# Row blocks of 112 and 16 for 1, 111 and 16 in a relu and row-sum kernel

## Chip, cores, metric

One core of one Trainium2 chip. The metric is device time in microseconds (us) of one execution, median of several; the span of a profile is about 1.4 us shorter than the time of its run. All runs told here are of the fast state, at a granted clock of 1.0. In the profile's lines SPq is the queue that issues the DMA transfers, ACT is ScalarE and DVE is VectorE. A load has landed when the last part of its data is in; a chunk is 16 rows per partition.

## The reference

The input x has the shape 32 x 512 x 1024 in float32, 16,384 rows of 1024 numbers, 67.1 MB.

```python
def reference(x: np.ndarray) -> np.ndarray:
    relu_x = np.maximum(x, 0)
    return np.sum(relu_x, axis=-1).astype(np.float32)
```

## The kernel before

The rows are laid on 128 partitions, 128 rows each. Which rows a partition gets is set by REGIONS: a block of n rows per partition takes 128 n consecutive rows of the input, and partition p the n rows from p x n of them. Before, there were three blocks of 1, 111 and 16 rows. So the very first load, one row per partition, is one contiguous piece of 512 KB. The price is that the sums of those 128 rows lie in one column, 4 bytes in each of 128 partitions, while the output has them side by side. The kernel transposes that column on VectorE and stores it as 4 pieces of 128 bytes.

```python
REGIONS = [1, 111, 16]
CHUNKS = [[(0, 0, 1), (1, 0, 15)]] + [[(1, 16 * c + 15, 16)] for c in range(6)]
# ... (block, first row, rows): chunk 0 is two loads, chunks 1 to 6 are one each
    xv = [
        xr[P * s : P * (s + n), :].rearrange("(p j) d -> p j d", p=P)
        for s, n in zip(start, REGIONS)
    ]
# ... three buffers of 16 rows; a load waits until VectorE has summed the chunk three before
    for c in range(NBIG + 1):
        if c >= NB:
            sp.wait_ge(s_dve, done[c - NB])
        if c < NBIG:
            i = 0
            for g, j, n in CHUNKS[c]:
                sp.dma_start(
                    out=buf[:, c % NB, i : i + n, :], in_=xv[g][:, j : j + n, :]
                ).then_inc(s_in[c], 16)
                i += n
# ... the loads of chunk 0 are moved ahead of the first barrier; tail loads of 8, 4, 2 rows;
# ... the last two rows come in four pieces, one of them (the end of the one row and the
# ... start of the other) into a tile of its own, "seam"
    sp.wait_ge(s_turn, 1)
    sp.dma_start(
        out=of[0:P].rearrange("(k q) -> k q", q=32), in_=turned[0:P:32, 0:32]
    ).then_inc(s_store, 16)
    sp.wait_ge(s_fact, 1)
    sp.wait_ge(s_fdve, 1)
    sp.wait_ge(s_in[-1], 16)
    sp.dma_start(out=ov[1][:, :], in_=res[:, start[1] : start[2]]).then_inc(s_store, 16)
# ... ScalarE applies relu to a chunk in place, VectorE sums its rows in steps:
        if c == 1:
            dve.wait_ge(s_dve, done[c])
            dve.transpose(out=turned[:, :], in_=res[:, 0:32]).then_inc(s_turn, 1)
```

Of the kernel before, what the change touches and what calls it, by code (L numbers as in the profile page):

```python
# [3 lines left out]
P = 128  # L4
D = 1024
BIG = 16
NB = 3
REGIONS = [1, 111, 16]
CHUNKS = [[(0, 0, 1), (1, 0, 15)]] + [[(1, 16 * c + 15, 16)] for c in range(6)]
ACT_STEPS = [[16], [7, 9], [7, 9], [7, 9], [4, 5, 7], [3, 4, 5]]  # L10
DVE_STEPS = [[4, 5, 7], [7, 4, 5], [7, 4, 5], [7, 4, 5], [4, 5, 7], [3, 4, 5]]
TAIL = [8, 4, 2]
CUT = 912
HEAD = 256


def bass_relu_sum_kernel(
# [1 line left out]
    x: bass.AP,  # L19
    out: bass.AP,  # L20
):




# [6 lines left out]
    fp32 = mybir.dt.float32  # L32
# [5 lines left out]
    J = B * S // P  # L38
    NBIG = len(CHUNKS)
    assert BIG * NBIG + sum(TAIL) + 2 == J == sum(REGIONS)  # L40

    xr = x.rearrange("b s d -> (b s) d")
    of = out.rearrange("b s -> (b s)")
    start = [sum(REGIONS[:i]) for i in range(len(REGIONS))]
# [4 lines that stand above are left out]
    ov = [of[P * s : P * (s + n)].rearrange("(p j) -> p j", p=P) for s, n in zip(start, REGIONS)]  # L49

    buf = nc.alloc_sbuf_tensor("buf", [P, NB, BIG, D], fp32)
    w = D - CUT
    seam = nc.alloc_sbuf_tensor("seam", [P, 2 + w + HEAD + 2], fp32)
    res = nc.alloc_sbuf_tensor("res", [P, J], fp32)
    turned = nc.alloc_sbuf_tensor("turned", [P, 32], fp32)

    n_in = NBIG + len(TAIL) + 3
    s_in = [nc.alloc_semaphore(f"s_in{i}") for i in range(n_in)]
# [1 line left out]
    s_dve = nc.alloc_semaphore("s_dve")  # L60
    s_fact = nc.alloc_semaphore("s_fact")
    s_fdve = nc.alloc_semaphore("s_fdve")
    s_half = nc.alloc_semaphore("s_half")
    s_seam = nc.alloc_semaphore("s_seam")
    s_last = nc.alloc_semaphore("s_last")
    s_turn = nc.alloc_semaphore("s_turn")
    s_store = nc.alloc_semaphore("s_store")
    s_out = nc.alloc_semaphore("s_out")

    sp, act, dve = nc.sync, nc.scalar, nc.vector  # L70

    NTWO = len(ACT_STEPS)
    done = [sum(map(len, DVE_STEPS[: c + 1])) for c in range(NTWO)]

# [10 lines left out]
# [8 lines that stand above are left out]
# [14 lines left out]

    rows = xv[-1].rearrange("p j d -> p (j d)")[:, r * D : (r + 2) * D]
    flat = buf[:, tb, r : r + 2, :].rearrange("p j d -> p (j d)")
    first, second, third = [(0, CUT), (D + D // 2, 2 * D), (D + HEAD, D + D // 2)]  # L110
    for k, (lo, hi) in enumerate((first, second, third)):
        sp.dma_start(out=flat[:, lo:hi], in_=rows[:, lo:hi]).then_inc(  # L112
            s_in[NBIG + len(TAIL) + k], 16
        )
    sp.dma_start(out=seam[:, 2 : 2 + w + HEAD], in_=rows[:, CUT : D + HEAD]).then_inc(s_seam, 16)
    sp.wait_ge(s_turn, 1)
    sp.dma_start(
        out=of[0:P].rearrange("(k q) -> k q", q=32), in_=turned[0:P:32, 0:32]
    ).then_inc(s_store, 16)
    sp.wait_ge(s_fact, 1)  # L120
    sp.wait_ge(s_fdve, 1)
    sp.wait_ge(s_in[-1], 16)
    sp.dma_start(out=ov[1][:, :], in_=res[:, start[1] : start[2]]).then_inc(s_store, 16)


    def on_act(t, acc):
        return act.activation(t, t, AF.Relu, accum_out=acc)  # L127

    def on_dve(t, acc):
        return dve.tensor_scalar(  # L130
            out=t, in0=t, scalar1=0.0, scalar2=None, op0=ALU.max, op1=ALU.add, accum_out=acc
        )

    def row(c, i):
        return buf[:, c % NB, i, :], res[:, c * BIG + i : c * BIG + i + 1]

    k = 0
    for c in range(NTWO):
        alone = BIG - sum(ACT_STEPS[c])
        act.wait_ge(s_in[c], 16 * len(CHUNKS[c]))  # L140
        r = 0
        ready = []
        for n in ACT_STEPS[c]:
            t = buf[:, c % NB, r : r + n, :]
            act.activation(t, t, AF.Relu).then_inc(s_act, 1)  # L145
            k += 1
            ready += [k] * n
            r += n
        for i in range(BIG - alone // 2, BIG):
            on_act(*row(c, i))  # L150
        if alone:
            dve.wait_ge(s_in[c], 16 * len(CHUNKS[c]))
            for i in range(BIG - alone, BIG - alone // 2):
                on_dve(*row(c, i))
        r = seen = 0
        for n in DVE_STEPS[c]:
            if ready[r + n - 1] > seen:
                seen = ready[r + n - 1]
                dve.wait_ge(s_act, seen)
            dve.tensor_reduce(  # L160
                out=res[:, c * BIG + r : c * BIG + r + n],
                in_=buf[:, c % NB, r : r + n, :],
                axis=X,
                op=ALU.add,
            ).then_inc(s_dve, 1)
            r += n
        if c == 1:
            dve.wait_ge(s_dve, done[c])
            dve.transpose(out=turned[:, :], in_=res[:, 0:32]).then_inc(s_turn, 1)  # L169


    j0 = NBIG * BIG
    for c in range(NTWO, NBIG):
        act.wait_ge(s_in[c], 16 * len(CHUNKS[c]))
        dve.wait_ge(s_in[c], 16 * len(CHUNKS[c]))
        for i in range(BIG):
# [10 lines left out]
    lo, hi = first  # L187
    act.wait_ge(s_in[-3], 16)
    dve.wait_ge(s_in[-3], 16)
    on_act(flat[:, lo : CUT // 2], seam[:, 0:1]).then_inc(s_half, 1)  # L190
    on_dve(flat[:, CUT // 2 : hi], seam[:, 1:2]).then_inc(s_half, 1)
    k = 2 + w
    lo, hi = second
    act.wait_ge(s_in[-2], 16)
    on_act(flat[:, lo:hi], seam[:, k + HEAD : k + HEAD + 1]).then_inc(s_seam, 1)
    lo, hi = third
    dve.wait_ge(s_in[-1], 16)
    on_dve(flat[:, lo:hi], seam[:, k + HEAD + 1 : k + HEAD + 2]).then_inc(s_seam, 1)
    act.wait_ge(s_seam, 16 + 2)
    act.wait_ge(s_half, 2)  # L200
    on_act(seam[:, 0:k], res[:, J - 2 : J - 1]).then_inc(s_last, 1)
    dve.wait_ge(s_seam, 16 + 2)
    on_dve(seam[:, k : k + HEAD + 2], res[:, J - 1 : J]).then_inc(s_last, 1)


    sp.wait_ge(s_last, 2)
    sp.dma_start(out=ov[-1][:, :], in_=res[:, start[-1] : J]).then_inc(s_out, 16)
    sp.wait_ge(s_store, 16 * (len(REGIONS) - 1))
    sp.wait_ge(s_out, 16)
# [28 lines left out]
```

## Time and profile before

| | before |
|---|---|
| time, median of 6 runs (range) | 160.83 us (160.75 to 161.05) |
| span of the profile | 159.4 us |
| first chunk landed | 21.61 us |
| mean step between the landings of chunks 0 to 6 | 19.35 us for 8.39 MB |
| last store issued | 157.93 us |

The rows that carry these, and how they are read, are in the prediction. This is the time of the first load from issue to landing (last column), from the page's list of DMA issues of the kernel before:

```profile
buf<-in_x_dram SPq DMA_DIRECT2D x1, 512.0 KB, 3.3
```

And these are the packets that the DMA began in the first 3 us of the span:

```profile
DMA packets 160, 1.51 MB, mean 502 GB/s; under 512 B 16, under 2 KB 16, under 8 KB 144
```

### The profile page before, as it was taken

The numbers are of one execution on the slowest core, as the hardware profiler recorded it, in microseconds if no ns is written. First come the engines' busy times: TensorE is split into PE (matmuls) and PEld (weight loads), VectorE is DVE, ScalarE is ACT, GpSimd is POOL, SyncE is SP. The second block draws the span as 40 slices with busy tenths as digits, with TensorE's granted clock in tenths as the row PEclk, the third lists the DMA queues.
The fourth block names the chain that finished last, engine by engine and source line by source line (L and its number), as shares of the span: only waits on it lengthen the run. The fifth ranks groups of instructions, "written<-read, shape, count | busy, mean of one in ns | idle before, by whom it ended". The sixth has DMA issues, their size and how long they took to land.

```text
span 159.4 us, 150 instructions
## 1 busy us (share of the span) xinstructions
DVE 120.6 (76%) x59; ACT 101.5 (64%) x54; POOL 0.2 (0%) x4
## 2 busy tenths in 40 slices
DVE  0000000009999999999999999999999999898995
ACT  3000059980799708996099941999329980496975
POOL 0000000000000000000000000000000000000000
DMA  9997996996996997989979969969969979798994
GB/s 378 493 401 339 493 526 263 526 526 263 526 493 296 526 444 345 526 378 411 526 312 477 526 263 526 526 263 526 526 263 526 444 345 526 321 469 374 417 400 142
DMA packets 2457, 67.18 MB, mean 421 GB/s; under 512 B 536, under 2 KB 792, under 8 KB 1176
## 3 DMA queue, kind: packets, MB, share of 16 engines
q1 hardware_dynamic: 2456, 67.18, 98.1%
q14 instruction: 1, 0.01, 0.0%
HBM read 67.11 MB, written 0.07 MB: 421 GB/s over the span
## 4 chain that ended last, share of the span: by engine, by line
DVE 55%; DMA 34%; ACT 9%; SPq 2%; issue 0%
DVE res L160 54%; DMA buf<-in_x_dram 34%; ACT buf L145 9%; SPq L101 1%; SPq L112 1%; DVE buf L130 0%; DVE seam L130 0%; SPq L91 0%; DVE turned L169 0%
## 5 line engine op out<-in xcount | busy, mean ns | idle before, releaser
L160 DVE TENSOR_REDUCE res<-buf 128x4 f32<-128x4096 f32 (+3 forms) x18 | 99.4, 5596 | 35.5 <-ACT buf L145 35.5
L145 ACT ACTIVATE buf<-buf 128x7168 f32<-128x7168 f32 (+5 forms) x13 | 80.4, 6233 | 46.1 <-DMA buf<-in_x_dram 46.1
L127 ACT ACTIVATE buf<-buf 128x1024 f32<-128x1024 f32 (+2 forms) x19 | 19.0, 999 | 8.9 <-DMA buf<-in_x_dram 8.9
L130 DVE TENSOR_SCALAR_CACHE_REDUCE buf<-buf 128x1024 f32<-128x1024 f32 (+2 forms) x19 | 20.7, 1143 | 1.7 <-DMA buf<-in_x_dram 1.6
L127 ACT ACTIVATION_READ_ACCUMULATOR buf<-buf 128x1 f32 x19 | 3.6, 188 | 0.0
L145 ACT ACT_TABLE_LOAD x1 | 1.3, 1283 | 1.3 <-PEq L223 1.3
L130 DVE DVE_READ_ACCUMULATOR buf<-buf 128x1 f32 x19 | 1.6, 84 | 0.0
L130 DVE TENSOR_SCALAR_CACHE_REDUCE seam<-seam 128x258 f32<-128x258 f32 x1 | 0.4, 421 | 0.0
L127 ACT ACTIVATE seam<-seam 128x114 f32<-128x114 f32 x1 | 0.3, 300 | 0.1
L169 DVE STREAM_TRANSPOSE turned<-res 128x32 f32<-128x32 f32 x1 | 0.2, 211 | 0.0
L127 ACT ACTIVATION_READ_ACCUMULATOR seam<-seam 128x1 f32 x1 | 0.2, 186 | 0.0
L223 POOL MEMSET const-bfloat16-1.0<- 128x1 bf16 x1 | 0.1, 101 | 0.0
L223 POOL MEMSET const-uint8-127<- 128x1 uint8 x1 | 0.1, 101 | 0.0
L223 POOL MEMSET const-float32-0.0<- 128x1 f32 x1 | 0.1, 98 | 0.2 <-issue 0.2
L223 POOL MEMSET const-float32-1.0<- 128x1 f32 x1 | 0.1, 98 | 0.0
L130 DVE DVE_READ_ACCUMULATOR seam<-seam 128x1 f32 x1 | 0.1, 82 | 0.0
## 6 DMA issues: line engine op xcount, KB each, us to landing
buf<-in_x_dram SPq DMA_DIRECT2D x1, 7680.0 KB, 21.1
buf<-in_x_dram SPq DMA_DIRECT2D x1, 4096.0 KB, 25.3
buf<-in_x_dram SPq DMA_DIRECT2D x1, 2048.0 KB, 29.9
buf<-in_x_dram SPq DMA_DIRECT2D x1, 1024.0 KB, 31.9
buf<-in_x_dram SPq DMA_DIRECT2D x1, 512.0 KB, 3.3
buf<-in_x_dram SPq DMA_DIRECT2D x1, 456.0 KB, 32.5
buf<-in_x_dram SPq DMA_DIRECT2D x1, 256.0 KB, 32.7
seam<-in_x_dram SPq DMA_DIRECT2D x1, 184.0 KB, 32.6
```

The source lines that it names most:

```text
L101: sp.dma_start(out=buf[:, tb, r : r + n, :], in_=xv[-1][:, r : r + n, :]).then_inc(s_in[NBIG + i], 16)
L112: sp.dma_start(out=flat[:, lo:hi], in_=rows[:, lo:hi]).then_inc(s_in[NBIG + len(TAIL) + k], 16)
L127: return act.activation(t, t, AF.Relu, accum_out=acc)
L130: return dve.tensor_scalar(out=t, in0=t, scalar1=0.0, scalar2=None, op0=ALU.max, op1=ALU.add, accum_out=acc)
L145: act.activation(t, t, AF.Relu).then_inc(s_act, 1)
L160: dve.tensor_reduce(out=res[:, c * BIG + r : c * BIG + r + n], in_=buf[:, c % NB, r : r + n, :], axis=X, op=ALU.add,).then_inc(s_dve, 1)
L169: dve.transpose(out=turned[:, :], in_=res[:, 0:32]).then_inc(s_turn, 1)
L223: nc = _bacc.Bacc("TRN2", target_bir_lowering=False, num_devices=1)
```

## The change

The intent: a simpler layout, with one block of 112 rows and no column that needs transposing, and pieces of the last two rows that begin and end on multiples of 512 bytes. The first load is still one row per partition, but of 112; its 128 pieces of 4 KB now lie 448 KiB apart.

```diff
-REGIONS = [1, 111, 16]
-CHUNKS = [[(0, 0, 1), (1, 0, 15)]] + [[(1, 16 * c + 15, 16)] for c in range(6)]
+REGIONS = [112, 16]
+CHUNKS = [[(0, 0, 1), (0, 1, 15)]] + [[(0, 16 * c, 16)] for c in range(1, 7)]
-DVE_STEPS = [[4, 5, 7], [7, 4, 5], [7, 4, 5], ...
+DVE_STEPS = [[4, 5, 7], [3, 4, 4, 5], [7, 4, 5], ...
-CUT = 912
+CUT = 896
+MID = 512                      # the same place as D // 2 before
-    seam = nc.alloc_sbuf_tensor("seam", [P, 2 + w + HEAD + 2], fp32)
+    z = 96
+    seam = nc.alloc_sbuf_tensor("seam", [P, z + w + HEAD + 2], fp32)
-    sp.dma_start(out=seam[:, 2 : 2 + w + HEAD], in_=rows[:, CUT : D + HEAD]).then_inc(s_seam, 16)
-    sp.wait_ge(s_turn, 1)
-    sp.dma_start(
-        out=of[0:P].rearrange("(k q) -> k q", q=32), in_=turned[0:P:32, 0:32]
-    ).then_inc(s_store, 16)
+    sp.dma_start(out=seam[:, z : z + w + HEAD], in_=rows[:, CUT : D + HEAD]).then_inc(s_seam, 16)
-    sp.dma_start(out=ov[1][:, :], in_=res[:, start[1] : start[2]]).then_inc(s_store, 16)
+    sp.dma_start(out=ov[0][:, :], in_=res[:, 0 : start[1]]).then_inc(s_store, 16)
-        if c == 1:
-            dve.wait_ge(s_dve, done[c])
-            dve.transpose(out=turned[:, :], in_=res[:, 0:32]).then_inc(s_turn, 1)
...                             # the tile and semaphore of the transpose, and seam offsets
```

More of the change, by code (lines that the diff above doesn't have):

```diff
@@ L7 @@
 NB = 3
-REGIONS = [1, 111, 16]
-CHUNKS = [[(0, 0, 1), (1, 0, 15)]] + [[(1, 16 * c + 15, 16)] for c in range(6)]
+REGIONS = [112, 16]
+CHUNKS = [[(0, 0, 1), (0, 1, 15)]] + [[(0, 16 * c, 16)] for c in range(1, 7)]
 ACT_STEPS = [[16], [7, 9], [7, 9], [7, 9], [4, 5, 7], [3, 4, 5]]
-DVE_STEPS = [[4, 5, 7], [7, 4, 5], [7, 4, 5], [7, 4, 5], [4, 5, 7], [3, 4, 5]]
+DVE_STEPS = [[4, 5, 7], [3, 4, 4, 5], [7, 4, 5], [7, 4, 5], [4, 5, 7], [3, 4, 5]]
 TAIL = [8, 4, 2]
-CUT = 912
+CUT = 896
 HEAD = 256
+MID = 512
 def bass_relu_sum_kernel(
@@ L52, in bass_relu_sum_kernel @@
     w = D - CUT
-    seam = nc.alloc_sbuf_tensor("seam", [P, 2 + w + HEAD + 2], fp32)
+    z = 96
+    seam = nc.alloc_sbuf_tensor("seam", [P, z + w + HEAD + 2], fp32)
     res = nc.alloc_sbuf_tensor("res", [P, J], fp32)
-    turned = nc.alloc_sbuf_tensor("turned", [P, 32], fp32)
     n_in = NBIG + len(TAIL) + 3
@@ L65, in bass_relu_sum_kernel @@
     s_last = nc.alloc_semaphore("s_last")
-    s_turn = nc.alloc_semaphore("s_turn")
     s_store = nc.alloc_semaphore("s_store")
@@ L109, in bass_relu_sum_kernel @@
     flat = buf[:, tb, r : r + 2, :].rearrange("p j d -> p (j d)")
-    first, second, third = [(0, CUT), (D + D // 2, 2 * D), (D + HEAD, D + D // 2)]
+    first, second, third = [(0, CUT), (D + MID, 2 * D), (D + HEAD, D + MID)]
     for k, (lo, hi) in enumerate((first, second, third)):
@@ L189, in bass_relu_sum_kernel @@
     dve.wait_ge(s_in[-3], 16)
-    on_act(flat[:, lo : CUT // 2], seam[:, 0:1]).then_inc(s_half, 1)
-    on_dve(flat[:, CUT // 2 : hi], seam[:, 1:2]).then_inc(s_half, 1)
-    k = 2 + w
+    on_act(flat[:, lo : CUT // 2], seam[:, z - 2 : z - 1]).then_inc(s_half, 1)
+    on_dve(flat[:, CUT // 2 : hi], seam[:, z - 1 : z]).then_inc(s_half, 1)
+    k = z + w
     lo, hi = second
@@ L200, in bass_relu_sum_kernel @@
     act.wait_ge(s_half, 2)
-    on_act(seam[:, 0:k], res[:, J - 2 : J - 1]).then_inc(s_last, 1)
+    on_act(seam[:, z - 2 : k], res[:, J - 2 : J - 1]).then_inc(s_last, 1)
     dve.wait_ge(s_seam, 16 + 2)
```

## The prediction

> **What bounds the kernel now.** I read the page first, then the queue's own waits, then the order of instructions on each engine. On the page:
>
> ```profile
> span 159.4 us, 150 instructions
> DVE 120.6 (76%) x59; ACT 101.5 (64%) x54; POOL 0.2 (0%) x4
> ...
> DMA packets 2457, 67.18 MB, mean 421 GB/s; under 512 B 536, under 2 KB 792, under 8 KB 1176
> ...
> q1 hardware_dynamic: 2456, 67.18, 98.1%
> ...
> DVE 55%; DMA 34%; ACT 9%; SPq 2%; issue 0%
> ```
>
> Two readings compete. The chain of work that ended last gives 55% to VectorE, but the one hardware DMA queue is busy for 98.1% of the span and VectorE for 76%. The chain is followed back through "buffer free, so the load was issued"; whether that wait cost anything depends on how much was still queued when the load was issued. The order of instructions tells this. The starts of ScalarE are the landings of the loads (the releaser in brackets is the load), and the SP rows are the issues:
>
> ```profile
> 21.61 13.86 ACT L145 ACTIVATE buf<-buf 128x16384 f32<-128x16384 f32 x1 [19.06 <-DMA buf<-in_x_dram]
> 40.97 13.95 ACT L145 ACTIVATE buf<-buf 128x7168 f32<-128x7168 f32 x2 [5.50 <-DMA buf<-in_x_dram]
> ...
> 118.36 10.63 ACT L145 ACTIVATE buf<-buf 128x3072 f32<-128x3072 f32 x3 [5.31 <-DMA buf<-in_x_dram]
> ...
> 137.72 1.06 ACT L127 ACTIVATE buf<-buf 128x1024 f32<-128x1024 f32 x1 [6.65 <-DMA buf<-in_x_dram]
> ```
> ```profile
> 104.82 0.33 SPq L91 DMA_DIRECT2D buf<-in_x_dram  x1
> 122.07 1.28 SPq L101 DMA_DIRECT2D buf<-in_x_dram  x3
> 123.39 1.43 SPq L112 DMA_DIRECT2D buf<-in_x_dram  x3
> 124.87 0.44 SPq L115 DMA_DIRECT2D seam<-in_x_dram  x1
> 125.35 0.63 SPq L117 DMA_DIRECT2D out_dram<-turned  x1
> ```
>
> The last 16-row chunk was issued at 104.82, while the chunk before it landed only at 118.36: 13.5 us of transfers were still queued. The tail was issued at 122.07, and the chunk ahead of it landed at 137.72: 15.7 us queued. So a buffer that comes free a few tenths of a us earlier or later changes nothing. The landings are equidistant: (137.72 - 21.61)/6 = 19.35 us for each 8.39 MB, or 433.5 GB/s. The kernel is a stream at a fixed rate. Its time is a start (the first chunk lands at 21.61, which is 19.35 of streaming plus 2.26), the stream, and what follows the last byte:
>
> ```profile
> 157.01 0.42 DVE L130 TENSOR_SCALAR_CACHE_REDUCE buf<-buf 128x256 f32<-128x256 f32 x1 [0.40 <-DMA buf<-in_x_dram]
> 157.08 0.34 SPq L123 DMA_DIRECT2D out_dram<-res  x1
> ...
> 157.47 0.30 ACT L127 ACTIVATE seam<-seam 128x114 f32<-128x114 f32 x1
> 157.47 0.42 DVE L130 TENSOR_SCALAR_CACHE_REDUCE seam<-seam 128x258 f32<-128x258 f32 x1
> 157.68 0.19 ACT L127 ACTIVATION_READ_ACCUMULATOR seam<-seam 128x1 f32 x1
> 157.82 0.08 DVE L130 DVE_READ_ACCUMULATOR seam<-seam 128x1 f32 x1
> 157.93 0.34 SPq L207 DMA_DIRECT2D out_dram<-res  x1
> ```
>
> The last small loads land near 157.0 to 157.47, the seam takes until 157.90, and the last store (1.4 us from issue to landing) ends the span.
>
> **What the Trainium skill says.** All of it is in "DMA: Bandwidth & Descriptors". (1) Section "Where 436 GB/s comes from": the ports of SBUF carry 435.2 GB/s. The 433.5 measured here agrees, so there is hardly anything left to gain from the stream. (2) Section "Latency and other measured facts", row on HBM row pitch at large powers of two: per-partition pitches of 512 KiB and more lose rate (207 GB/s against 214 at 512 KiB, 103 at 4 MiB), and a few KiB of padding restores it. The changed kernel moves the pitch from 111 to 112 rows, 444 to 448 KiB, which is seven times 64 KiB. No pitch of 448 KiB is in this trace, but the tail has one of 64 KiB. (3) Section "How a descriptor splits into AXI transactions": a descriptor that doesn't start on 256 bytes fetches from the boundary below. This trace doesn't show it singly. (4) Section "Queues, rings and completion order": each engine takes descriptors in ring order. The trace agrees: loads issued at 122 to 125 land in order of issue, some 25 to 33 us later.
>
> **The change part by part.**
>
> *The first load becomes one row of the block of 112, not a contiguous 512 KB.* It stays 128 pieces of 4 KB, now 448 KiB apart. Before, it landed 3.3 us after issue; at 433.5 GB/s its 524,288 bytes would take 1.2 us, so most is latency. In the first 3 us the DMA moves 1.51 MB in 160 packets, and its rate is ragged for the first half us of data. Scattered rows could make that ramp a little slower; a delay there shifts the whole stream by the same amount. I allow 0 to +0.2 us, middle +0.05.
>
> *Pitch 448 KiB in the big chunks.* A loss of 1% in rate would cost 116.11 x 1% = 1.2 us between the first and the seventh chunk, so this is the largest lever. The tail answers it: its pitch is 16 rows = 64 KiB, where all 128 partitions start at the same offset modulo 64 KiB just as they will at 448 KiB. Eight tail rows (4.19 MB) land in 147.43 - 137.72 = 9.71 us, 432.0 GB/s, 0.35% under the chunks, with the switch between DMAs included. If all of that were due to the pitch, seven chunks would lose 135 x 0.35% = 0.5 us; I think most of it is not, and take +0.05.
>
> *No transposed store.* On VectorE the transpose stood between a reduction ending at 64.61 + 5.47 = 70.08 and the next starting at 70.25: 0.17 us. That goes away. The DMA loses four packets of data and, I expect, four completion packets: 2457 to 2449. The store was issued at 125.35 behind all loads in the same queue, so it ran after them and before the end; it delayed no load. It did not end last either. Gain on the path: 0.
>
> *Second chunk summed as 3, 4, 4, 5 rows for 7, 4, 5.* Durations by shape: 3.354 + 4.413 - 7.605 = +0.162 us. But neighbouring reductions overlap: the first six took 2 x (4.413 + 5.480 + 7.605) = 35.00 by sum and 34.58 by the clock, 0.07 each. So about +0.09. With the transpose gone VectorE is 0.17 - 0.09 = 0.08 us earlier, against 13 us of queue: nothing. It also waits 0.42 us for the last chunk at 137.72, which would swallow the same amount in the other direction.
>
> *The cut at 896 and the aligned seam.* The bytes of the last two rows are the same in sum; 64 bytes per partition move from the first piece to the seam. Before, the seam's source began 3648 bytes into the row, 64 past a 256-byte boundary, and its destination 8 bytes into its tile; now both start on round offsets. By the skill's account that saves fetching 64 bytes more for each of 8 seam descriptors per engine, 0.02 us at one engine's share of 433.5/16 = 27 GB/s (estimate, from that section); allowing as much for the destination, 0.04 us at the end of the stream. Work after landing: the first piece is halved at 448 for 456, ahead of a wait. ScalarE's seam piece grows from 114 to 130 elements, 16 x (1045 - 630)/512 = 13 ns, and ends at 157.88 rather than 157.87; VectorE's, unchanged at 258, ends at 157.90 and still decides. Gain: 0.04.
>
> *Stores.* The big one grows from 55.5 to 56 KB, 448 bytes per partition for 444, evenly spaced at multiples of 64; it is issued 0.85 us before the last. Its packets may go slightly faster; the last store waits for its own landing. I take -0.02.
>
> Sum: +0.05 +0.05 +0 +0 -0.04 -0.02 = +0.04 us on 160.83, so 160.87. The before runs spread over 0.22 us, so no digit beyond the first means anything: 160.8 to 160.9.
>
> **Rivals.** (a) *Pitch aliasing.* With 448 KiB all 16 engines run through the same offsets in step, as large powers of two do. For it: at 444 KiB they were staggered by 12 rows modulo 16, and perhaps the odd block of 111 was chosen for that. Against it: the tail's 432.0 GB/s at 64 KiB, and the skill's own loss at 512 KiB is only 7 of 214. Taking that 3.3% in full, 7 x 19.35 x 3.3% = 4.5 us, 165.3 us; I give it 2%. A partial loss of 0.3% gives 161.2. (b) *The start gets better or worse.* If the contiguous load was a real benefit and scattered rows run at half rate for 1.2 us, +1.2 us, 162.0; against it, small tail pieces with scattered rows keep (1.05 MB in 154.84 - 152.32) 416 GB/s. If the shorter ramp comes from spreading over more of HBM, -0.3 us, 160.5. (c) *VectorE is the bound, as the chain's 55% suggests.* Then the time would fall by 0.08 us, 160.75: not to be told from nothing. (d) *The ragged end costs more than I think*, so that aligned pieces and the missing store give 0.2 to 0.4 us: the stream's rate from 154.84 to 157.47 was 1.05 MB / 2.63 = 399 GB/s against 433.5, so at most 0.21 us is there to be had. 160.6.
>
> **Range and chances.** All likely outcomes lie within 0.3% of before; a 2% change needs 3.2 us, which only rival (a) reaches. The range takes in (d), a start that is 0.3 us either way, and a slight pitch loss: 160.4 to 161.3. Faster by over 2%: 0.01. Within: 0.97. Slower: 0.02.
>
> **What would show it.** In the changed kernel's profile: seven landings 19.35 us apart (19.4 or more says pitch); the first chunk landing at 21.6 to 21.7 (later says start); 2449 packets; the queue of loads still over 13 us deep at the last buffer wait; VectorE ending its reductions within 0.1 us of 137.3; the last store issued 0.4 to 0.5 us after the last VectorE piece begins. I am wrong if the landings move apart, or the first chunk or the last seam moves by over half a us.

## The result

The changed kernel takes 161.01 us, median of 6 runs (160.88 to 161.39), against 160.83 (160.75 to 161.05). The ratio is 1.0014, 95% interval 1.0001 to 1.0026. Here and below a ratio is the mean time of one kernel's fast runs over that of the other's of the same rounds, so not quite the ratio of the medians. By the 2% measure it is the same; within that, it is slower by some 0.2 us, with an interval that only just leaves out no difference at all.

The page of the changed kernel, the lines that answer to those of before:

```profile
span 159.5 us, 149 instructions
DVE 120.5 (76%) x59; ACT 101.5 (64%) x54; POOL 0.2 (0%) x4
...
DMA packets 2449, 67.18 MB, mean 421 GB/s; under 512 B 528, under 2 KB 784, under 8 KB 1168
...
buf<-in_x_dram SPq DMA_DIRECT2D x1, 512.0 KB, 3.6
```

The eight packets have gone as expected, nothing else has moved except the last line: the first load lands 3.6 us after its issue for 3.3. What the DMA began in the first 3 us of the span has fallen from 1.51 to 1.13 MB: 125 pieces of the first load for 128, and 10 large ones of the second for 16:

```profile
DMA packets 145, 1.13 MB, mean 375 GB/s; under 512 B 10, under 2 KB 10, under 8 KB 135
```

The order of ScalarE's instructions, whose starts are the landings:

```profile
21.74 13.86 ACT L141 ACTIVATE buf<-buf 128x16384 f32<-128x16384 f32 x1 [19.20 <-DMA buf<-in_x_dram]
41.09 13.95 ACT L141 ACTIVATE buf<-buf 128x7168 f32<-128x7168 f32 x2 [5.49 <-DMA buf<-in_x_dram]
...
137.84 1.06 ACT L123 ACTIVATE buf<-buf 128x1024 f32<-128x1024 f32 x1 [6.64 <-DMA buf<-in_x_dram]
```

The first chunk is 0.13 us late (21.74 for 21.61). The step is (137.84 - 21.74)/6 = 19.35 us, as before, so the pitch of the large loads costs nothing that this shows. The lateness is carried along unchanged: 0.12 at the seventh chunk. The end, and the loads that wait for a buffer:

```profile
104.79 0.33 SPq L91 DMA_DIRECT2D buf<-in_x_dram  x1
122.04 1.28 SPq L101 DMA_DIRECT2D buf<-in_x_dram  x3
...
158.04 0.34 SPq L200 DMA_DIRECT2D out_dram<-res  x1
```

From the seventh chunk to the last store it is 158.04 - 137.84 = 20.20 us against 20.21. The tail is issued 0.03 us earlier than before although the stream started 0.13 later; VectorE did gain, and it bought nothing. All of the difference between these two traces is there when the first chunk has landed. It is 0.1 us: the profiled execution of the changed kernel took 160.88 us, as little as any of its six.

### The profile page after: what moved, and what is told of

Same layout as the page of the kernel before. It is cut to its first block, busy times and chain, and to the rows that moved or that the text cites. A ratio compares the mean times of both kernels' runs of the same rounds, so it can differ in the third digit from the quotient of the medians.

```text
span 159.5 us, 149 instructions
## 1 busy us (share of the span) xinstructions
DVE 120.5 (76%) x59; ACT 101.5 (64%) x54; POOL 0.2 (0%) x4
## 2 busy tenths in 40 slices
DMA packets 2449, 67.18 MB, mean 421 GB/s; under 512 B 528, under 2 KB 784, under 8 KB 1168
## 4 chain that ended last, share of the span: by engine, by line
DVE 55%; DMA 34%; ACT 9%; SPq 2%; issue 0%
DVE res L156 54%; DMA buf<-in_x_dram 34%; ACT buf L141 9%; SPq L101 1%; SPq L112 1%; DVE buf L126 0%; DVE seam L126 0%; SPq L91 0%
```

## The experiments

Each ran beside the kernel before on the same chip, which took 160.76 in the first group, 160.81 in the second and 160.82 in the third (medians of 9 runs each). Of each other kernel there are five runs, six of the store without the transpose, four where it is said. A kernel that reads wrong rows moves the same bytes; where only 128 of 16,384 sums are affected, the comparison with the reference still passes.

My theory S: the 0.2 us come from the first load, whose pieces no longer lie together. Rivals: P, the pitch of 448 KiB in the large loads; A, only pitches that are multiples of 64 KiB are bad; E, something at the end.

### Make the first load contiguous in the changed kernel

```diff
-    in_=xv[g][:, j : j + n, :]
+    in_=xr[0:P, :].rearrange("(p j) d -> p j d", p=P) if (c, i) == (0, 0) else xv[g][:, j : j + n, :],
```

> The changed kernel, only its first load reads the first 128 rows of the input in one contiguous piece (wrong rows, so a wrong result on purpose); the pitch of 448 KiB in all else stays. Theory S (the 0.18 us are lost in the first load, because its 128 pieces of 4 KB lie apart): first landing of a chunk back at 21.6 us, 160.8 us. Rival P (the pitch of 448 KiB in the large loads costs it): stays at 161.0. Rival E (the end: cut, seam, larger store): stays at 161.0.

160.88 us, five runs from 160.80 to 160.89, ratio 1.0001 (0.9987 to 1.0015). The time is as S has it, to within about 0.1. The trace was not: the first load landed in 3.3 us as before, but the first chunk only at 21.76, no earlier than in the changed kernel (21.74), and S had 21.6.

```profile
buf<-in_x_dram SPq DMA_DIRECT2D x1, 512.0 KB, 3.3
```
```profile
21.76 13.86 ACT L142 ACTIVATE buf<-buf 128x16384 f32<-128x16384 f32 x1 [19.22 <-DMA buf<-in_x_dram]
```

Both profiled executions took 160.88 us, so these two traces can't tell the kernels apart. A single trace's first chunk varies by a tenth, so it can't carry a verdict about 0.1 us alone. The landing of the first load is steadier: over all traces of this document it takes 3.3 to 3.4 us where the load is one contiguous row, and 3.5 to 4.5 where it is scattered. Everything else of the change is in this kernel, so all other parts together, the missing store included, come to nothing that five runs can resolve. That is not very sharp: the interval is 0.2 us to either side, as wide as the loss. More telling is that none of these five runs is over 160.89, and none of the eleven of the changed kernel (six above, five below, in other rounds) is under 160.88.

### Scatter the first load in the kernel before

```diff
-    in_=xv[g][:, j : j + n, :]
+    in_=xv[1][:, 0:1, :] if (c, i) == (0, 0) else xv[g][:, j : j + n, :],
```

> The kernel before, only its first load reads one row of each partition's 111 (pitch 444 KiB, wrong rows on purpose). Theory S: the first chunk lands at 21.75, 161.0 us. Theory A (scattering is harmless, only a pitch of a multiple of 64 KiB is bad, because all pieces then share their low address bits): 160.83, as before, first chunk at 21.6. Rivals P and E: 160.83.

161.15 us (160.95 to 161.25), ratio 1.0019 (1.0006 to 1.0031). No run of it is as fast as the slowest of the contiguous version on the same chip (160.89), though two of the nine of the kernel before there were not either (161.03 and 161.14). Of this kernel's DMA issues and of ScalarE's order:

```profile
buf<-in_x_dram SPq DMA_DIRECT2D x1, 512.0 KB, 4.0
```
```profile
22.12 13.86 ACT L146 ACTIVATE buf<-buf 128x16384 f32<-128x16384 f32 x1 [19.57 <-DMA buf<-in_x_dram]
```

One edit to the first load gives the kernel before the whole loss, and somewhat more. Rivals P and E had no loss here, and are not needed to explain one; A falls: 444 KiB is not a multiple of 64 KiB and is no better than 448.

It was run again in the third group, with the changed kernel beside it:

> The kernel before with the scattered first load again (pitch 444 KiB, wrong rows on purpose): 161.0 to 161.2, with the changed kernel and not with the kernel before.

161.15 us again (160.94 to 161.28), ratio 1.0018; first load 3.9 us, first chunk at 22.05.

> The changed kernel again, on the chip of these runs: 161.0, 0.1 to 0.3 above the kernel before, and with a wider spread than its.

161.03 us (160.93 to 161.06), ratio 1.0011 (0.9999 to 1.0024), first load 3.6 us. The loss by scattering repeats on another chip, and the changed kernel is again some 0.2 us behind. The wider spread that I expected did not: in the first set it had been 0.5 us, here it is 0.13.

### Only the cut and the seam

The kernel before with CUT at 896 and the seam at offset 96 of its tile, as in the change.

> The kernel before with only the cut at 896 and the seam at its aligned place (result correct). My prediction's term: -0.04 us, so 160.8, and from the seventh chunk's landing (137.7) to the issue of the last store 20.17 instead of 20.21 us. Rival E: 160.9 to 161.0.

160.78 us (160.67 to 160.81), ratio 0.9995 (0.9982 to 1.0007). The trace has 157.92 - 137.73 = 20.19 us from the seventh chunk to the last store, 0.02 less than before; I had put -0.04 on it. It is the fastest version here by the median and it is not to be told from the kernel before.

### No small first load

```diff
-CHUNKS = [[(0, 0, 1), (0, 1, 15)]] + ...
+CHUNKS = [[(0, 0, 16)]] + ...
```

> The changed kernel with chunk 0 in one load of 16 rows instead of 1 and 15 (result correct). If the small first load serves to start the stream early, this loses some tenths: 161.2 to 161.8, first chunk at 21.9 or later. If what costs time is the latency of many small scattered pieces, one load of 64 KB pieces has no such pieces and gets 160.8 or better.

161.05 us (160.89 to 161.17), ratio 1.0012 (0.9999 to 1.0025); first chunk at 22.01. Neither expectation met its number: the time lies between them, level with the changed kernel. So, as far as 0.2 us can be told here, the small first load helps only as a contiguous one; scattered over 128 places it is worth no more than none at all.

### How far apart

The changed kernel with the first load's rows 2 and 16 rows apart in the place of 112.

> The changed kernel, only its first load reads every second row of the first 256 (pitch 8 KiB, all within 1 MiB; wrong rows on purpose). Theory D (what counts is how far apart the 128 pieces lie, that is how many distinct regions of HBM are touched cold): as contiguous, 160.8 to 160.9. Theory N (any gap between the pieces costs it): 161.0 to 161.2.

162.22 us (162.10 to 162.26, four runs), ratio 1.0085: neither theory. This is the worst place of all, though all its pieces lie within 1 MiB:

```profile
buf<-in_x_dram SPq DMA_DIRECT2D x1, 512.0 KB, 4.5
```
```profile
23.16 13.86 ACT L142 ACTIVATE buf<-buf 128x16384 f32<-128x16384 f32 x1 [20.63 <-DMA buf<-in_x_dram]
```

> The changed kernel, only its first load reads one row in sixteen of the last block (pitch 64 KiB, all within 8 MiB; wrong rows on purpose). Theory D: between, 160.85 to 161.0. Theory N: 161.0 to 161.2. If low address bits in common were the trouble after all, as bad as 448 KiB or worse, 161.0 to 161.4.

161.16 us (161.01 to 161.41), ratio 1.0020; first load 3.5 us, first chunk at 21.86. Its trace is of its slowest run (161.41). There the first chunk is 0.25 us late, and another 0.4 us went in the middle of the stream (four steps of 19.40 to 19.52), which I can't explain. So not all of what 64 KiB cost need be lost at the start.

So distance (theory D) is not the rule: 8 KiB costs 1.4 us, 64 and 444 KiB about 0.35, 448 about 0.2. That any gap costs something (N) holds in direction and fails on size at 8 KiB. Which property of the address decides stays open. What the traces do show is how the loss reaches the end. The semaphore of a load counts 16 completions, as many as the core has DMA engines; their times are in the trace, though no view prints them:

| first load | completions of chunk 1, first and last (us) | of the seam, at the end |
|---|---|---|
| kernel before, contiguous | 40.43, 40.94 | 156.98, 157.44 |
| changed kernel, 448 KiB | 40.57, 41.07 | 157.10, 157.54 |
| 444 KiB | 40.69, 41.44 | 157.22, 157.93 |
| 8 KiB | 41.07, 42.49 | 157.55, 158.88 |

The spread between first and last is still there at the end, less 0.1 us at most. I read this as each engine having its own share of every load and keeping the lateness of its first pieces; the records don't name the engine, so this is not shown singly. The wait is for the last. At 444 and 8 KiB the last completion is later by more than the first is. In the changed kernel itself it is not so: the spread is no wider than before (0.50 for 0.51), and the first and the last completion came 0.14 and 0.13 us later together.

### Is it the start or the small pieces?

Chunk 0 in 16 loads of one row, scattered and contiguous.

```diff
-CHUNKS = [[(0, 0, 1), (0, 1, 15)]] + ...
+CHUNKS = [[(0, j, 1) for j in range(16)]] + ...
```

> The changed kernel with chunk 0 in 16 loads of one row, each in 128 pieces of 4 KB at a pitch of 448 KiB (result correct). Theory R (only the first pieces of the cold start are slow; after that the queue hides it): within 0.3 us of the changed kernel, 160.9 to 161.3. Theory T (small scattered pieces run at a lower rate throughout): 16 times the loss of 0.15 us, 163 us or more, first chunk at 24.

> The same with each of the 16 loads of chunk 0 contiguous, 512 KB each (wrong rows on purpose). Theory R: 160.8 to 161.0, 0.1 to 0.3 us below the scattered form. Theory T: 160.8, over 2 us below it.

162.31 us (162.13 to 162.61, four runs) scattered and 162.28 (162.14 to 162.82) contiguous; the second is wrong by the comparison. Both numbers are outside both expectations, but the difference of the two decides: if scattered pieces ran slower throughout, the scattered form would be over 2 us behind, and it is 0.03 behind. So Theory T falls. That the scatter costs at the start, as R has it, is not seen here: the 0.1 to 0.3 us that R wanted between the two forms are missing as well. Pieces of 4 KB in a whole chunk cost both forms alike some 1.3 us against the changed kernel, which I had not foreseen. In the contiguous form's trace, which is of its slowest run, the completions of chunk 1 were 1.4 us apart, and 0.7 in the scattered form's; here being contiguous did not keep them together.

### Store the first column without the transpose

What was the transposed store for? The kernel before, without the transpose, its 128 sums stored straight from the column:

```diff
-    sp.wait_ge(s_turn, 1)
-    sp.dma_start(
-        out=of[0:P].rearrange("(k q) -> k q", q=32), in_=turned[0:P:32, 0:32]
-    ).then_inc(s_store, 16)
+    sp.wait_ge(s_dve, done[1])
+    sp.dma_start(out=ov[0][:, :], in_=res[:, 0 : start[1]]).then_inc(s_store, 16)
```

> The kernel before without the transpose: the 128 sums of its first block are stored as 128 pieces of 4 bytes, issued where the transposed store was (result correct). If that store runs behind all loads and ahead of the end, as I said of the transposed one, it costs at most the time of 8 small packets per engine between the last load and the last store: 160.8 to 161.1, first chunk at 21.6. If small stores at the end hold up the last one: 161.2 or more.

166.77 us (165.81 to 167.26), ratio 1.0379: nearly 6 us slower, and far beyond what I expected. Of the waits of the queue and of the DMA issues of this kernel:

```profile
SPq L204 <- DMA out_dram<-res: 5.6, 1, 5.6
```
```profile
out_dram<-res SPq DMA_DIRECT2D x1, 55.5 KB, 6.6
out_dram<-res SPq DMA_DIRECT2D x1, 0.5 KB, 35.7
out_dram<-res SPq DMA_DIRECT2D x1, 8.0 KB, 5.9
```

The loads are nearly as fast as before (first chunk at 21.60, the seventh at 137.93 for 137.72). The small store of 0.5 KB stands behind the loads in the queue, as I had said of the transposed one. But 128 pieces of 4 bytes then hold up the stores behind them: the last store takes 5.9 us to land instead of 1.4, and the final wait is 5.6 us instead of 1.1.

> The same with a first block of two rows per partition, so a contiguous first load of 1 MB in pieces of 8 KB, blocks of 2, 110 and 16 rows (result correct). If one contiguous row is all that the start needs: 160.8 to 161.1, as the version with one. If a longer contiguous start helps more: 160.6. If a longer small-piece phase costs: 161.1 or more.

163.34 us (163.29 to 163.37, four runs), ratio 1.0156; first chunk at 21.75. Pieces of 8 bytes hold up the end by less, the final wait is 3.0 us. Whether a longer contiguous start is better the time can't tell, with 2 us lost at the end; the trace has no sign of it.

## Why the prediction was right

The measured 161.01 lies in the range, and "within 2%" was right, for the reason given: the kernel is a stream at a fixed rate and the change touches it hardly. The sum in its text came to 160.87, and the measured time is 0.14 above. Two errors nearly cancel in that: 0.05 allowed for the pitch, of which the step shows nothing, and 0.06 of gain at the end, of which no run shows anything clear. What is left is the first load, put about 0.15 too small. By its steps:

- **First load: mechanism right, size too small.** I allowed 0 to +0.2 us with a middle of +0.05. The first load landed 0.3 us later in the trace and the first chunk 0.13; at 21.74 it is just past the 21.6 to 21.7 that I had set ("later says start"). The runs say about 0.2: the changed kernel at 1.0014 and 1.0011 of before, and 1.0001 once its first load is contiguous again. This is the term of the sum that was mis-sized. "Shifts the whole stream by the same amount" is what the changed kernel's trace has. What I had not thought of is that the engines can lose unequally, as they do at 444 and 8 KiB, where the last of them decides. And I misread the 1.51 MB: they had been begun in the first 3 us, not moved.
- **Pitch of the large loads, +0.05.** The step stayed 19.35 us, so 0 as far as a trace can tell. The tail's 64 KiB rows had been a good witness for the stream. They were a bad one for the start: rival (b) leaned on the same tail to say that scattered rows keep their rate, and in mid-stream they do. (A slip in rival (a): 111 rows are 15 modulo 16; the 12 are KiB modulo 16 KiB.)
- **No transposed store, 0 on the path.** Borne out as part of the contiguous version (1.0001); no run took it away alone. The 2449 packets came out. My reading that its four packets ran behind the loads and harmed nothing holds for 128-byte pieces only: as 128 pieces of 4 bytes the same 512 bytes cost 6 us.
- **VectorE, 0.08 us earlier.** Its chain from the first reduction to the tail's issue took 86.39 us in place of 86.55, so 0.16. I had counted the 0.17 of the transpose but not that two reductions now meet there and overlap, by the 0.07 to 0.08 that neighbours do. Off the path, as said: the tail issued 0.03 us earlier and ended 0.11 later.
- **Cut and seam, -0.04; stores, -0.02.** Seventh chunk to last store: 20.20 for 20.21, and 20.19 with the cut and the seam alone. The sign agrees, but the size is below what a trace can tell.
- **The rivals.** (a) fell with the unchanged step. (c), VectorE as the bound, fell with its gain that bought nothing. (d), an end that had been costing 0.2 to 0.4 us, has nothing for it: the cut and the seam alone gained nothing that shows (0.9995, 0.9982 to 1.0007). (b) is what came, at a sixth of the 1.2 us that it had put on it; at a pitch of 8 KiB the loss was 1.4.

Left open: which property of the addresses sets the cost of a scattered start, and whether the contiguous version still lags the kernel before (0.12 us by the medians of its group, 0.02 by the means), which the runs can't separate from nothing.

## What to carry to other kernels

Where a kernel is one stream at a fixed rate, look at the first pieces of the first load: in these traces what was late at the start was late at the end, and nothing made it good. Layout of the input and layout of the output pull against each other here: the contiguous first row was worth 0.2 us and needed a transpose to avoid stores of 4 bytes that would cost 6; the change gives up the 0.2 and with them the need for the transpose, a fair trade for simpler code. When a trace of one part of a kernel is called as a witness for another, ask whether a deep queue hid in the one what shows in the other.

## What the Trainium skill lacked or had wrong

- "DMA: Bandwidth & Descriptors", section "Latency and other measured facts", has the loss by row pitch for large powers of two from 512 KiB up, in copies between HBM tensors in tiles of 16 KiB rows. The runs show a loss at a cold start for other pitches too, in one load of 128 pieces of 4 KB: about 1.4 us of device time at a pitch of 8 KiB, 0.35 at 444 KiB and 0.2 at 448 KiB, against a contiguous load, and 0.35 at 64 KiB, there perhaps not all at the start.
- The same page, in "Specifications", says that transfers under 512 B fall below line rate, and gives no time for it. As the runs show it, 512 bytes of output cost nothing visible as 4 pieces of 128 bytes, and nearly 6 us as 128 pieces of 4 bytes: the last store, queued behind them, took 5.9 us to land for 1.4.
- No page that I read says that differences between the engines at the start stay for a whole kernel: 0.5 us between the first and the last completion of a load at 41 us and still at 157 us, and 1.4 and 1.3 us in the worst version.
- "Where 436 GB/s comes from", on the same page, agreed: 435.2 stated, 433.5 measured in the stream.
